# A two-layer encoder trunk: feed-forward products by Strassen's seven block products, with two of the weight sums made by accumulating DMA

## The chip, the core and the metric

One core of one Trainium2 chip runs the kernel. The number to predict is the device time of one execution in microseconds (us). Before the change three runs took 2454.03, 2454.52 and 2454.72 us; the median, 2454.52 us, is the time before.

Engine names are those of the profile: PE is TensorE with its matmuls, PEld its weight loads, DVE is VectorE, ACT is ScalarE, POOL is GpSimd, SP is SyncE, which issues the DMAs of this kernel.

## What is computed

The reference runs two layers on 512 tokens of width 1024. Cut to what matters here:

```python
D_MODEL, SEQ, DEPTH, D_FF = 1024, 512, 2, 2816

def swiglu(x, w_up, w_down):
    a, b = jnp.split(x @ w_up, 2, axis=-1)
    return (jax.nn.silu(a) * b) @ w_down

for i in range(DEPTH):
    x = layer_norm(ALPHA * x + 0.5 * swiglu(x, ffn1_up[i], ffn1_down[i]), ln1_g[i], ln1_b[i])
    mix = token_mix(x, w_in[i], ...)          # four token mixers, gates, an output product
    x = layer_norm(ALPHA * x + mix, ln2_g[i], ln2_b[i])
    ple = jax.nn.sigmoid(x @ w_ple_gate[i]) * (p[i] @ w_ple[i])
    x = layer_norm(ALPHA * x + 0.5 * swiglu(x, ffn2_up[i], ffn2_down[i]) + ple, ln3_g[i], ln3_b[i])
```

The four SwiGLU feed-forwards (two in each layer) are what the change touches.

## The kernel before

Every dense product is three passes of float32r matmuls: an operand is split into hi = float32r(x), by an ACT cast, and lo = x - hi, by a DVE subtract (`split`, L127 to L129), and lo*hi + hi*lo + hi*hi is accumulated (`mm3`, L112 to L116). Weights come by `weights` (L104): one DMA of 512 KB into a `stage` buffer (three of them), then the split into `whi` and `wlo` (six each).

A feed-forward has 22 blocks of 128 hidden features. For a block the up product makes the a half and the b half, each 8 row blocks x 3 passes with 512 token columns, 48 matmuls in all; `finish` (L318) then makes silu on ACT, the product on DVE (`hm`, L324) and the split into `h`. Blocks are taken in two chunks, of 10 and of 12. After a chunk's up products come its down products, a loop over column halves, in it over pairs of blocks, in it over the four token tiles: a pair costs 48 matmuls with 512 columns too. Their sums are added to the rows `z`. The last down product feeds the layer norm, whose transposes are woven between matmuls.

The order on PE is the order of the program text. On the other engines a scheduler sets the order; each engine runs its own list strictly in that order, and DMAs are issued from SP's list. In the second feed-forward of a layer, `ple` (the per-layer embedding) comes first; it needs `pT`, loaded and split by `load_p`, and the rows `z`, which `load_rows` reads back from the scratch `xs` where the norm before stored them.

Of the kernel before, what the change touches and what calls it, by code (L numbers as in the profile page):

```python
# [26 lines left out]
CHUNKS = ((0, 10), (10, 22))  # L27
T2 = 7
# [49 lines left out]
class Trunk:  # L78
    """Every dense product runs as three float32r passes: an operand x is split exactly into
    hi = float32r(x) and lo = x - hi, and lo*hi + hi*lo + hi*hi is accumulated in float32.  # L80
    Activations are kept feature-major (hi and lo, [feature, token]); residuals and layer norms
    are token-major."""

    def __init__(self, tc, ctx, t):
        self.tc, self.nc, self.t = tc, tc.nc, t
        pool = lambda *a, **k: ctx.enter_context(tc.tile_pool(*a, **k))
        self.const = pool(name="const", bufs=1)
        self.ring = pool(name="ring", bufs=1)
        self.small = pool(name="small", bufs=4)
# [7 lines left out]
        self.st, self.ln = {}, []  # L97
        self.scratch = [self.dram.tile([P, D], F32, tag=f"xs{i}", name=f"xs{i}") for i in range(NT)]
        self.w = Weave()
# [4 lines left out]
    def weights(self, src, n=1024):  # L104
        s = self.ring.tile([P, 1024], F32, tag="stage", name="stage", bufs=3)
        h = self.ring.tile([P, 1024], F32R, tag="whi", name="whi", bufs=6)
        lo = self.ring.tile([P, 1024], F32R, tag="wlo", name="wlo", bufs=6)
        self.nc.sync.dma_start(out=s[:, :n], in_=src)
        self.split(h[:, :n], lo[:, :n], s[:, :n])
        return h, lo  # L110

    def mm3(self, ps, lh, ll, rh, rl, start, stop):  # L112
        mm = self.nc.tensor.matmul
        mm(ps, lh, rl, start=start, stop=False)  # L114
        mm(ps, ll, rh, start=False, stop=False)  # L115
        mm(ps, lh, rh, start=False, stop=stop)  # L116
# [24 lines left out]
    def begin(self, up, fp):  # L141
        """The first two pairs of products, in the order in which their operands arrive."""
        ws = [[self.ring.tile([P, 1024], F32R, tag=q, name=q, bufs=6) for q in ("whi", "wlo")] for _ in range(4)]
        raw = [fp.tile([P, 1024], F32, tag="h", name=f"w0_{q}", bufs=12) for q in range(4)]
        ps = [self.bank("up") for _ in range(4)]
        warm = fp.tile([P, SEQ], F32R, tag="h", name="warm", bufs=12)
        self.nc.vector.memset(warm.bitcast(F32), 0.0)
        for _ in range(12):
            self.nc.tensor.matmul(ps[3], warm[:, :P], warm, start=True, stop=True)
        for kk in range(KD // 2):  # L150
            c = slice(256 * kk, 256 * kk + 256)
            x = fp.tile([P, 2, SEQ], F32, tag="h", name=f"x0_{kk}", bufs=12)

            def weight(q):
                self.nc.sync.dma_start(out=raw[q][:, c], in_=up[q // 2, q % 2][:, c])
# [15 lines left out]
    def constants(self):  # L171
        self.load(self.ident, self.t["ident"])
        self.nc.gpsimd.memset(self.mhalf, -0.5)
        self.trig()

    def trig(self):
# [21 lines left out]
        with self.tc.tile_pool(name="trig", bufs=1) as tp:  # L198
            pi = tp.tile([P, NT], I32, tag="pi", name="pi")
            nc.sync.dma_start(out=pi, in_=t["pos"])  # L200
            fr = tp.tile([P, NF], F32, tag="fr", name="fr")
            nc.sync.dma_start(out=fr, in_=t["freq"].partition_broadcast(P))
            pf = tp.tile([P, NT], F32, tag="pf", name="pf")
            v.tensor_copy(pf, pi)
            mk = lambda n: tp.tile([P, NT, NF], F32, tag=n, name=n)
            r, k, s, e, m = mk("r"), mk("k"), mk("s"), mk("e"), mk("m")
# [15 lines left out]
            # angle = 65536 m + rest, and 65536 m = m (c1 + c2 + c3 + c4) mod 2 pi  # L222
# [39 lines left out]
    def norm(self, z, i, g, b, last):  # L262
# [14 lines left out]
        for j in range(2):  # L277
# [6 lines left out]
            self.split(self.xh[sl], self.xl[sl], ps)  # L284

# [10 lines left out]
    def ffn(self, l, which, res, last):  # L296
        nc, t = self.nc, self.t
        up, dn = t[f"up{which}"][l], t[f"dn{which}"][l]
        with ExitStack() as ctx:
            if which == 2:  # L300
                pp = ctx.enter_context(self.tc.tile_pool(name=f"ple{l}", bufs=1, reuse_waits="tile"))
                pt = self.load_p(l, pp)
            fp = ctx.enter_context(self.tc.tile_pool(name=f"ffn{l}{which}", bufs=1, reuse_waits="tile"))
            z = [fp.tile([P, D], F32, tag=f"z{i}", name=f"z{i}") for i in range(NT)]
            g, b = [fp.tile([P, D], F32, tag=q, name=q) for q in ("lng", "lnb")]

            def load_rows():
                self.load_res(z, res)
                self.load_gb(g, b, l, 1 if which == 1 else 3)

            if l or which == 2:
                load_rows()
            if which == 2:
                self.ple(l, z, pp, pt)
            lead = 2 if which == 1 else 0
            alpha = ALPHA2 if which == 1 else None
            h = {}

            def finish(tt, pa, pb):
                sa = fp.tile([P, SEQ], F32, tag="sa", name="sa", bufs=2)  # L320
                hm = fp.tile([P, SEQ], F32, tag="hm", name="hm", bufs=2)
                ht = fp.tile([P, 2, SEQ], F32R, tag="h", name="h", bufs=12)
                nc.scalar.activation(sa, pa, AF.Silu)  # L323
                nc.vector.tensor_tensor(hm, sa, pb, op=ALU.mult)  # L324
                self.split(ht[:, 0, :], ht[:, 1, :], hm)
                h[tt] = ht

            def accumulate(i, half, ps):
                zs = z[i][:, half * 512:(half + 1) * 512]
                if alpha is not None and first:  # L330
                    nc.vector.scalar_tensor_tensor(zs, zs, alpha, ps, op0=ALU.mult, op1=ALU.add)
                else:
                    nc.vector.tensor_tensor(zs, zs, ps, op=ALU.add)
                if tail:
                    self.stats(z[i], i, half)

            for ci, (k0, k1) in enumerate(CHUNKS):
                first, tail = ci == 0, ci == len(CHUNKS) - 1
                tt = k0
                if first and lead:  # L340
                    if l == 0:
                        ps = self.begin(up, fp)
                    else:
                        ws = [self.weights(up[q // 2, q % 2]) for q in range(4)]
                        ps = [self.bank("up") for _ in range(4)]
                        for c0 in (0, 256):
                            self.ready(c0 // P, c0 // P + 1)
                            for w, p in zip(ws, ps):
                                self.up_mm(p, w, c0, c0 + 256)
                    for q in range(lead):  # L350
                        finish(q, ps[2 * q], ps[2 * q + 1])
                    tt = lead
                while tt < k1:
                    if l == 0 and which == 1 and tt == lead + 2:
                        self.constants()
                        load_rows()
                    ps = []
                    for ab in range(2):
                        w = self.weights(up[tt, ab])
                        p = self.bank("up")  # L360
                        self.up_mm(p, w, 0, SEQ)
                        ps.append(p)
                    finish(tt, *ps)
                    tt += 1
                for half in range(2):
                    ps = [self.bank(f"dn{i}") for i in range(NT)]
                    pairs = list(range(k0 // 2, k1 // 2))
                    late = pairs[-LATE:] if tail and half else []

                    def mm(pr, w, i):  # L370
                        for j in range(2):
                            k = 2 * pr + j
                            s, m = slice(i * P, (i + 1) * P), slice(j * 512, (j + 1) * 512)
                            self.mm3(ps[i], h[k][:, 0, s], h[k][:, 1, s], w[0][:, m], w[1][:, m],
# [561 lines left out]
```

## Time and profile before

| | |
|---|---|
| median of the runs | 2454.52 us |
| span of the profiled execution | 2452.4 us |
| PE busy | 2443.3 us (100%), 10996 matmuls |
| DVE busy | 1083.5 us (44%) |
| ACT busy | 695.5 us (28%) |
| POOL busy | 55.1 us (2%) |
| DMA | 257 MB, mean 105 GB/s |

The span runs from the first to the last instruction of one profiled execution. The execution as it is timed also has some 2.1 us around it: the median is that much longer than the span. Because matmuls are pipelined, a matmul's duration (0.39 us for 512 columns) is longer than the distance from one start to the next; the distance is what adds up to the time. It is read from the number of matmuls in a stretch, or from two starts.

### The profile page before, as it was taken

Reading aid. Unit: us, or ns where it says so; the run is one execution under the profiler, and the core shown is the slowest. Engines: PE = TensorE matmul, PEld = TensorE weight load, DVE = VectorE, ACT = ScalarE, POOL = GpSimd, SP = SyncE. Lnnn points to the kernel's source line nnn. Section 1 sums busy time; section 2 is a strip of 40 time slices with the busy share of each in tenths; the row PEclk is TensorE's granted clock in tenths of the full one; section 3 lists DMA queues with packets and bytes.
Section 4 is the critical chain, followed back from the end, with each engine's and each line's share of the span. In section 5 each row is a group of like instructions: output and inputs, shape, how many; then the busy total and the mean of one; then the engine's idle time right before and its main releaser. Section 6 shows DMA issues by size and latency. Waiting matters only on the chain.

```text
span 2452.4 us, 26924 instructions
## 1 busy us (share of the span) xinstructions
PE 2443.3 (100%) x10996; PEld 1987.5 (81%) x10996; DVE 1083.5 (44%) x1712; ACT 695.5 (28%) x994; POOL 55.1 (2%) x93
## 2 busy tenths in 40 slices
PE   9999999999999999999999999999999999999998
PEld 7888888888888888888888888888888888888886
DVE  6333348545446533333443333485454464333334
ACT  4212214324232322222232222143342323222220
POOL 0000001000000000000000000010000000000000
PEclk9999999999999999999999999999999999999999
DMA  6323324213322533322352333232223234333331
GB/s 235 96 92 95 93 95 130 85 58 103 129 95 103 171 96 96 93 95 95 95 174 93 94 94 95 95 121 85 79 91 129 95 114 161 95 94 95 95 95 52
DMA packets 76939, 257.22 MB, mean 105 GB/s; under 512 B 10384, under 2 KB 13584, under 8 KB 76816
## 3 DMA queue, kind: packets, MB, share of 16 engines
q1 hardware_dynamic: 76816, 255.51, 32.4%
q8 instruction: 86, 1.41, 0.2%
q14 instruction: 37, 0.30, 0.0%
HBM read 242.89 MB, written 12.58 MB: 104 GB/s over the span
## 4 chain that ended last, share of the span: by engine, by line
PE 100%; DVE 0%; issue 0%; DVEq 0%
PE up L114 13%; PE up L115 13%; PE up L116 13%; PE dn L115 7%; PE dn L116 7%; PE dn L114 7%; PE gate L116 5%; PE gate L114 5%; PE gate L115 5%; PE wo L114 1%; PE pg L115 1%; PE wo L116 1%; PE pg L116 1%; PE pg L114 1%; PE wo L115 1%; PE br L116 1%
## 5 line engine op out<-in xcount | busy, mean ns | idle before, releaser
L129 DVE TENSOR_TENSOR wlo<-stage,whi 128x1024 fp32r<-128x1024 f32 (+1 forms) x416 | 505.3, 1215 | 728.9 <-ACT whi L128 728.5
L128 ACT CAST whi<-stage 128x1024 fp32r<-128x1024 f32 (+1 forms) x416 | 431.7, 1041 | 728.3 <-PE up L116 294.2
L114 PE MATMUL up<-xl,whi 128*128 128x512 f32 (+1 forms) x1440 | 562.6, 391 | 0.0
L116 PE MATMUL up<-xh,whi 128*128 128x512 f32 (+1 forms) x1440 | 562.2, 390 | 0.0
L115 PE MATMUL up<-xh,wlo 128*128 128x512 f32 (+1 forms) x1440 | 562.2, 390 | 0.0
L114 PEld LDWEIGHTS up<-xl,whi 128*128 128x128 f32 x1440 | 270.6, 188 | 63.3 <-DVE xl L129 0.6
L116 PEld LDWEIGHTS up<-xh,whi 128*128 128x128 f32 x1440 | 270.5, 188 | 62.5
L115 PEld LDWEIGHTS up<-xh,wlo 128*128 128x128 f32 x1440 | 270.6, 188 | 62.4
L114 PE MATMUL dn<-wlo,h 128*128 128x512 f32 x704 | 278.9, 396 | 0.0
L116 PE MATMUL dn<-whi,h 128*128 128x512 f32 x704 | 277.9, 395 | 0.0
L115 PE MATMUL dn<-whi,h 128*128 128x512 f32 x704 | 277.9, 395 | 0.0
L114 PE MATMUL gate<-xl,whi 128*128 128x512 f32 x512 | 206.0, 402 | 0.0
L116 PE MATMUL gate<-xh,whi 128*128 128x512 f32 x512 | 202.6, 396 | 0.0
L115 PE MATMUL gate<-xh,wlo 128*128 128x512 f32 x512 | 202.5, 396 | 0.0
L324 DVE TENSOR_TENSOR hm<-sa,up 128x512 f32<-128x512 f32 x88 | 60.5, 688 | 226.3 <-PE up L116 226.2
L116 PEld LDWEIGHTS dn<-whi,h 128*128 128x128 f32 x704 | 132.0, 188 | 32.2
L115 PEld LDWEIGHTS dn<-whi,h 128*128 128x128 f32 x704 | 132.1, 188 | 31.8
L114 PEld LDWEIGHTS dn<-wlo,h 128*128 128x128 f32 x704 | 132.0, 188 | 31.7
L323 ACT ACTIVATE sa<-up 128x512 f32<-128x512 f32 x88 | 52.6, 598 | 337.9 <-PE up L116 334.2
L116 PEld LDWEIGHTS gate<-xh,whi 128*128 128x128 f32 x512 | 96.2, 188 | 23.1
L115 PEld LDWEIGHTS gate<-xh,wlo 128*128 128x128 f32 x512 | 96.3, 188 | 21.2
L114 PEld LDWEIGHTS gate<-xl,whi 128*128 128x128 f32 x512 | 96.3, 188 | 21.0
(256 smaller groups left out, 2419.4 us busy)
## 6 DMA issues: line engine op xcount, KB each, us to landing
stage<-up_in SPq DMA_DIRECT2D x172, 512.0 KB, 3.6
stage<-dn_in SPq DMA_DIRECT2D x88, 512.0 KB, 3.6
stage<-wg_in SPq DMA_DIRECT2D x64, 512.0 KB, 3.4
xs<-z SPq DMA_DIRECT2D x20, 512.0 KB, 2.6
z<-xs SPq DMA_DIRECT2D x20, 512.0 KB, 6.8
stage<-wbr_in SPq DMA_DIRECT2D x16, 512.0 KB, 3.3
stage<-wo_in SPq DMA_DIRECT2D x16, 512.0 KB, 3.3
stage<-wpg_in SPq DMA_DIRECT2D x16, 512.0 KB, 3.4
```

Of the source, the lines that this page charges most:

```text
L114: mm(ps, lh, rl, start=start, stop=False)
L115: mm(ps, ll, rh, start=False, stop=False)
L116: mm(ps, lh, rh, start=False, stop=stop)
L128: self.nc.scalar.copy(hi, src)
L129: self.nc.vector.tensor_tensor(lo, src, hi.bitcast(F32), op=ALU.subtract)
L323: nc.scalar.activation(sa, pa, AF.Silu)
L324: nc.vector.tensor_tensor(hm, sa, pb, op=ALU.mult)
```

## The change

For 84 of the 88 blocks' up products (all but the first two blocks of each first feed-forward) and for 18 of the 22 blocks' down products in each feed-forward, the product is cut into 2 x 2 blocks, and seven block products with 256 columns take the place of eight. An up unit (`unit`) has seven products of 4 row blocks x 3 passes, 84 matmuls with 256 columns, where 48 with 512 columns were. A down group has seven products for two token tiles; the same 84 stand for 48 in a pair of blocks.

The block sums of the activations are made by `combine` on DVE and split (in `norm`, `begin` and `finish`); those of the up weights by `up_blocks`: `r` holds A11 and A12; `q` gets A21 twice by a plain DMA from SP, and then A11 and A22 are added to its halves by a DMA with `accum_op=ADD`, issued from POOL; `e` holds A22 and a DVE sum; a last DVE sum goes into `r`. Four splits follow. `dn_blocks` does the same for down weights with two accumulating DMAs. There are four `stage` buffers instead of three, and chunks of 6, 6, 6 and 4 blocks; the last chunk's down product (`down_last`) stays classical. `load_p` moves behind `load_rows`.

```diff
-CHUNKS = ((0, 10), (10, 22))
+CHUNKS = ((0, 6), (6, 12), (12, 18), (18, 22))
...
+    def stage(self):
+        return self.ring.tile([P, 1024], F32, tag="stage", name="stage", bufs=4)
...
+    def up_blocks(self, src):
...
+        r, q, e = self.stage(), self.stage(), self.stage()
+        two = lambda t: t.rearrange("p (b c) -> p b c", b=2)
+        self.load(two(r), src[:, 0:2, :])
+        self.load(two(q), src[:, 2:3, :].to_broadcast([P, 2, 512]))
+        self.load(e[:, :512], src[:, 3, :])
+        self.nc.gpsimd.dma_start(out=two(q), in_=src[:, 0::3, :], accum_op=ALU.add)
+        wr = self.halves(r, 1024)
+        wq = self.halves(q, 1024)
+        v.tensor_tensor(e[:, 512:], q[:, 512:], r[:, :512], op=ALU.add)
+        we = self.halves(e, 1024)
+        v.tensor_tensor(r[:, 512:], r[:, 512:], e[:, 512:], op=ALU.add)
+        wf = self.halves(r[:, 512:], 512)
...
+    def combine(self, t, b12, b21, b22):
...
+        v.tensor_tensor(t[:, 2], b22, b12, op=ALU.subtract)
+        v.scalar_tensor_tensor(t[:, 1], t[:, 0], -1.0, b22, op0=ALU.mult, op1=ALU.subtract)
+        v.scalar_tensor_tensor(t[:, 3], t[:, 1], -1.0, b21, op0=ALU.mult, op1=ALU.subtract)
...
+        product(X, "A11", "B11", True)
+        nc.scalar.copy(sn[:, 0], X)
+        product(Y, "S1", "T1", True)
+        nc.scalar.copy(sn[:, 2], Y)
+        product(X, "S2", "T2", False)
+        nc.scalar.copy(sn[:, 1], X)
+        product(Z, "A12", "B21", True)
+        tt(cc[:, :HT], Z, sn[:, 0], op=ALU.add)
+        product(X, "S3", "T3", False)
+        tt(nb, X, sn[:, 2], op=ALU.add)
+        product(Y, "S4", "B22", False)
+        tt(cc[:, HT:], Y, sn[:, 1], op=ALU.add)
+        product(X, "A22", "T4", False)
...
+            if odd:
+                v.tensor_tensor(f[:, 4], f[:, 1], f[:, 0], op=ALU.subtract)
+                self.combine(f[:, 4:], f[:, 0], f[:, 2], f[:, 3])
+                h[pr] = fp.tile([P, 2, 7, HT], F32R, tag="h", name="hb", bufs=3)
+                self.split(h[pr][:, 0], h[pr][:, 1], f[:, 1:])
...
-                self.ple(l, z, pp, pt)
+                with pool("ple") as pp:
+                    self.ple(l, z, pp, self.load_p(l, pp))
```

How the lists of the engines change is shown at three places. On SP before the embedding of the first layer's second feed-forward, the kernel before has (wple and wpg are the embedding's weights, xs the scratch that the norm stores, wo the weights of the product ahead of it):

```order
L108 DMA stage_5696<-wo_in 128x1024
L108 DMA stage_5900<-wple_in 128x1024
L132 DMA ps__5879<-pT_in 128x1024
L108 DMA stage_5948<-wpg_in 128x1024
L108 DMA stage_5954<-wpg_in 128x1024
```

and the changed kernel, at the same load of pT:

```order
L194 DMA xs2_75<-z2_6917 128x1024
L129 DMA stage_7919<-wpg_in 128x1024
L194 DMA z0_7646<-xs0_73 128x1024
L194 DMA z1_7647<-xs1_74 128x1024
L194 DMA z2_7648<-xs2_75 128x1024
L194 DMA ps__7657<-pT_in 128x1024
L129 DMA stage_7925<-wpg_in 128x1024
```

The load of pT moved from ahead of the norm's stores to behind the third store and the read-back of what it stored.

On DVE at the start of a down phase (up and cc, nb, sX are up results, h and hb the split activations, dn and dX the first down results), the kernel before has at the end of the first chunk of up products:

```order
L129 TENSOR_TENSOR wlo_983<-stage_981,whi_982 128x1024
L324 TENSOR_TENSOR hm_842<-sa_841,up_816 128x512
L129 TENSOR_TENSOR wlo_1013<-stage_1011,whi_1012 128x1024
L129 TENSOR_TENSOR h_843<-hm_842,h_843 128x512
L129 TENSOR_TENSOR wlo_1043<-stage_1041,whi_1042 128x1024
L324 TENSOR_TENSOR hm_911<-sa_910,up_885 128x512
```

and the changed kernel at the end of the second chunk:

```order
L472 SCALAR_TENSOR_TENSOR hf_1894<-sX_1922,cc_1926 128x256
L472 SCALAR_TENSOR_TENSOR hf_1894<-nb_1927,cc_1926 128x256
L191 TENSOR_TENSOR wlo_2142<-stage_2113,whi_2141 128x768
L246 TENSOR_TENSOR hf_1894<-hf_1894 128x256
L247 SCALAR_TENSOR_TENSOR hf_1894<-hf_1894 128x256
L191 TENSOR_TENSOR wlo_2167<-stage_2112,whi_2166 128x768
L248 SCALAR_TENSOR_TENSOR hf_1894<-hf_1894 128x256
L191 TENSOR_TENSOR hb_2025<-hf_1894,hb_2025 128x1792
L521 TENSOR_TENSOR z0_620<-z0_620,dX_2028 128x256
```

Where one subtract of 512 columns stood behind the gating, three sums, two weight subtracts and one subtract of 1792 columns stand now.

On SP and DVE in the middle of an up phase of the changed kernel (stage_2661 and stage_2786 are the q of two units that follow each other), SP has

```order
L194 DMA stage_2660<-up1_in 128x1024
L194 DMA stage_2661<-up1_in 128x2x512
L194 DMA stage_2662<-up1_in 128x512
L194 DMA stage_2785<-up1_in 128x1024
L194 DMA stage_2786<-up1_in 128x2x512
L194 DMA stage_2787<-up1_in 128x512
```

and DVE behind it, for the next unit (stage_2916 to stage_2918):

```order
L191 TENSOR_TENSOR wlo_2802<-stage_2787,whi_2801 128x1024
L294 TENSOR_TENSOR cc_2689<-sY_2686,sn_2688 128x256
L191 TENSOR_TENSOR wlo_2807<-stage_2785,whi_2806 128x512
L191 TENSOR_TENSOR wlo_2924<-stage_2916,whi_2923 128x1024
L472 SCALAR_TENSOR_TENSOR hf_2782<-sX_2685,cc_2689 128x256
L472 SCALAR_TENSOR_TENSOR hf_2782<-nb_2690,cc_2689 128x256
L191 TENSOR_TENSOR wlo_2928<-stage_2917,whi_2927 128x1024
L492 TENSOR_TENSOR hf_2782<-hf_2782 128x256
L144 TENSOR_TENSOR stage_2918<-stage_2917,stage_2916 128x512
```

Three stage buffers a unit are taken where two were, and the split of q (here wlo_2928) stands behind the gating of the unit on PE. The plain load of a q waits in the built program for the count that DVE gives after the subtract of the q before it: it gets that buffer.

## Rows read from the trace of the kernel before

**Rows 1.** The page's part 1: busy time, share, instructions.
```profile
PE 2443.3 (100%) x10996; PEld 1987.5 (81%) x10996; DVE 1083.5 (44%) x1712; ACT 695.5 (28%) x994; POOL 55.1 (2%) x93
```

**Rows 2.** The page's part 4: the chain that ended last, by engine.
```profile
PE 100%; DVE 0%; issue 0%; DVEq 0%
```

**Rows 3.** Busy time by stretch: engines with counts, clock, DMA share, GB/s.
```profile
100.00:150.00 50.00, 50.00 (x216) 40.14 (x215) 16.18 (x17) 11.46 (x13) 0.00 (x0) 1.00 0.30 92
...
1250.00:1300.00 50.00, 50.00 (x216) 40.27 (x215) 17.33 (x19) 13.91 (x18) 0.00 (x0) 1.00 0.35 106
```

**Rows 4.** PE in order of time, layer two's first up product: start, duration.
```profile
1225.19 0.28 PE L114 MATMUL up<-xl,whi 128*128 128x256 f32 x1
...
1226.14 0.28 PE L116 MATMUL up<-xh,whi 128*128 128x256 f32 x1
```

**Rows 5.** PE in order of time where the first down phase starts.
```profile
117.83 0.40 PE L116 MATMUL up<-xh,whi 128*128 128x512 f32 x1
118.06 0.40 PE L114 MATMUL dn<-wlo,h 128*128 128x512 f32 x1
```

**Rows 6.** DVE in order of time at the same place.
```profile
118.27 0.69 DVE L324 TENSOR_TENSOR hm<-sa,up 128x512 f32<-128x512 f32 x1 [2.75 <-PE up L116]
...
120.49 0.68 DVE L129 TENSOR_TENSOR h<-hm,h 128x512 fp32r<-128x512 f32 x1
```

**Rows 7.** DVE groups by form: busy us, mean ns, idle before.
```profile
L129 DVE TENSOR_TENSOR wlo<-stage,whi 128x1024 fp32r<-128x1024 f32 x404 | 493.8, 1223 | 718.4 <-ACT whi L128 718.0
...
L129 DVE TENSOR_TENSOR y<-yT,y 128x256 fp32r<-128x256 f32 x24 | 10.0, 415 | 16.9 <-ACT y L128 16.7
...
L560 DVE SCALAR_TENSOR_TENSOR cn<-mlap,rsrm,gn 128x256 f32<-128x256 f32 x8 | 3.9, 484 | 6.5 <-POOL rsrm L138 6.5
...
L129 DVE TENSOR_TENSOR wlo<-stage,whi 128x768 fp32r<-128x768 f32 x2 | 1.9, 959 | 10.5 <-ACT whi L128 10.5
...
L129 DVE TENSOR_TENSOR wlo<-stage,whi 128x512 fp32r<-128x512 f32 x2 | 1.4, 684 | 0.0
```

**Rows 8.** ACT groups by form.
```profile
L128 ACT CAST whi<-stage 128x1024 fp32r<-128x1024 f32 x404 | 421.7, 1047 | 728.2 <-PE up L116 294.2 <-PE dn L116 286.1 <-issue 70.9
L128 ACT CAST h<-hm 128x512 fp32r<-128x512 f32 x88 | 54.2, 616 | 8.6 <-DVE hm L324 8.6
```

**Rows 9.** SP's issues in order of time: start, duration of the group.
```profile
753.77 0.42 SPq L132 DMA_DIRECT2D ps__5879<-pT_in  x1
757.67 17.83 SPq L108 DMA_DIRECT2D stage<-wpg_in  x4
782.26 12.42 SPq L132 DMA_DIRECT2D xs<-z  x3
```

**Rows 10.** DMA issues: count, KB each, median us from issue to landing.
```profile
stage<-up_in SPq DMA_DIRECT2D x172, 512.0 KB, 3.6
...
xs<-z SPq DMA_DIRECT2D x20, 512.0 KB, 2.6
...
lnb<-ln_b_in SPq DMA_DIRECT2D x6, 512.0 KB, 9.5
...
ps__5879<-pT_in SPq DMA_DIRECT2D x1, 512.0 KB, 5.3
```

**Rows 11.** The tile pw: its matmuls, durations in ns, first and last start.
```profile
L114 PE MATMUL pw<-wlo,ph x32: 393/394/483, 796.1 to 2051.9; 128*128 128x512 f32 x32
```

**Rows 12.** Busy time by stretch where the DMA engines are full (columns as Rows 3).
```profile
1240.00:1245.00 5.00, 5.00 (x45) 5.00 (x44) 1.91 (x2) 2.31 (x3) 0.00 (x0) 1.00 1.01 406
```

**Rows 13.** POOL groups by form.
```profile
L138 POOL TENSOR_TENSOR rsln<-rsln,mhalf 128x1 f32<-128x1 f32 x24 | 22.5, 939 | 2065.8 <-DVE rsln L137 2065.8
```

**Rows 14.** Busy time by stretch at the end of the span.
```profile
2444.00:2448.00 4.00, 0.80 (x4) 0.31 (x2) 3.06 (x7) 0.00 (x0) 0.92 (x1) 1.00 0.34 126
2448.00:2452.00 4.00, 0.00 (x0) 0.00 (x0) 1.33 (x3) 0.00 (x0) 0.00 (x0) 0.56 0.35 131
```

More of the change, by code (lines that the diff above doesn't have):

```diff
@@ new lines, in close_tt, with xop, unit, product @@
+    def close_tt(self):
+        self.tt.close()
+        self.tt = None
+    def xop(self, c):
+        if c[0] == "T":
+            q = int(c[1]) - 1
+            return [(self.th[:, q, k, :], self.tl[:, q, k, :]) for k in range(HK)]
+        r, s = int(c[1]) - 1, int(c[2]) - 1
+        return [tuple(x[:, r * HK + k, s * HT:(s + 1) * HT] for x in (self.xh, self.xl)) for k in range(HK)]
+    def unit(self, w, tp):
+        nc = self.nc
+        X, Y, Z = [self.bank(q, [P, HT]) for q in ("sX", "sY", "sZ")]
+        sn = tp.tile([P, 3, HT], F32, tag="sn", name="sn", bufs=1)
+        cc = tp.tile([P, SEQ], F32, tag="cc", name="cc", bufs=2)
+        nb = tp.tile([P, HT], F32, tag="nb", name="nb", bufs=2)
+        tt = nc.vector.tensor_tensor
+        def product(ps, a, b, first):
+            for k, (rh, rl) in enumerate(self.xop(b)):
+                c = slice(k * P, (k + 1) * P)
+                self.mm3(ps, w[a][0][:, c], w[a][1][:, c], rh, rl, first and k == 0, k == HK - 1,
+                         skip_group_check=True)
+        product(X, "A11", "B11", True)
[11 more added lines that the diff above has]
+        product(X, "A22", "T4", False)
+        return cc, X, nb
@@ L260, in stats, with norm @@
         self.nc.vector.bn_stats(self.st[i][:, half, :], z[:, half * 512:(half + 1) * 512])
-    def norm(self, z, i, g, b, last):
+    def norm(self, z, i, g, b, last, blocks):
         nc = self.nc
@@ L284, in norm @@
             self.split(self.xh[sl], self.xl[sl], ps)
+            if not blocks or i < NT // 2:
+                continue
+            if j == 0:
+                self.w.need(self.ln[i - NT // 2])
+                t = self.temp("xt").rearrange("p (c k n) -> p c k n", c=4, k=HK)
+                sl = (slice(None), slice(0, HK), slice((i - 2) * P, (i - 1) * P))
+                nc.scalar.copy(t[:, 2], ps)
+                nc.vector.tensor_tensor(t[:, 0], self.xl[sl].bitcast(F32), ps, op=ALU.subtract)
+                nc.vector.tensor_tensor(t[:, 0], t[:, 0], self.xh[sl].bitcast(F32), op=ALU.add)
+            else:
+                sl = (slice(None), slice(HK, KD), slice((i - 2) * P, (i - 1) * P))
+                self.combine(t, t[:, 2], self.xh[sl].bitcast(F32), ps)
+                nc.vector.tensor_tensor(t[:, 3], t[:, 3], self.xl[sl].bitcast(F32), op=ALU.subtract)
+                sl = (slice(None), slice(None), slice(None), slice((i - 2) * P, (i - 1) * P))
+                self.split(self.th[sl], self.tl[sl], t)
     def ready(self, *toks):
@@ L297, in ffn @@
         nc, t = self.nc, self.t
[L298 to L305, printed above, removed]
+        v = nc.vector
@@ L307, in load_rows @@
+        up, dn, dnp = t[f"up{which}"][l], t[f"dn{which}"][l], t[f"dnp{which}"][l]
+        pool = lambda n: self.tc.tile_pool(name=f"{n}{l}{which}", bufs=1, reuse_waits="tile")
+        with pool("z") as zp:
+            first_use = l == 0 and which == 1
+            if first_use:
+                scratch = zp.tile([P, D], F32, tag="z3", name="trig")
+            z = []
             def load_rows():
+                z.extend(zp.tile([P, D], F32, tag=f"z{i}", name=f"z{i}") for i in range(NT))
                 self.load_res(z, res)
-                self.load_gb(g, b, l, 1 if which == 1 else 3)
@@ L311, in ffn @@
-            if l or which == 2:
+            if not first_use:
                 load_rows()
             if which == 2:
-                self.ple(l, z, pp, pt)
[L315 to L331, printed above, removed]
-                else:
[L333 to L374, printed above, removed]
-                                     k == k0, k == k1 - 1)
-                    for pr in pairs:
-                        if pr in late:
-                            continue
-                        w = self.weights(dn[pr, half])
-                        for i in range(NT):
-                            mm(pr, w, i)
-                    if late:
-                        ws = [self.weights(dn[pr, half]) for pr in late]
-                        self.ln = []
-                        for i in range(NT):
-                            for pr, w in zip(late, ws):
-                                mm(pr, w, i)
-                            accumulate(i, half, ps[i])
-                            self.ln.append(self.w.spawn(self.norm(z[i], i, g, b, last)))
-                    else:
-                        for i in range(NT):
-                            accumulate(i, half, ps[i])
```

231 lines of the change are left out of this document (198 added, 33 removed).

## The prediction

> **What bounds the kernel now.** I read the page's busy shares first, then the chain that ended last, then the stretches, and only then the groups by form, since the first three decide whether a row of another engine costs anything. The reader should see that PE is busy in the whole span and everything else is under half [rows 1], that the chain of waits is all PE and no other engine's line has a share [rows 2], and that an even 50 us of up products holds 216 matmuls, twice, far apart [rows 3]. So today the time is the number of matmuls times their distance: 50 / 216 = 0.2315 us with 512 columns. DVE and ACT stand between for 16 and 11 us of 50 and cost nothing. The kernel can therefore gain by fewer columns on PE, and it can lose whatever makes PE wait.
>
> **What PE saves.** The trace has a stretch with 256 columns, the start of layer two's first feed-forward. From the first to the ninth matmul there are 8 distances in 0.95 us, 0.1188 us each [rows 4]: slightly more than half of 0.2315. An up unit was 48 x 0.2315 = 11.11 us and becomes 84 x 0.1188 = 9.98 us, 1.13 us less (10%, not the eighth that the count of products promises). There are 84 such units, and 9 pairs of blocks in each of four feed-forwards have the same trade in their down products: 84 + 36 = 120 times 1.13 is 136 us. The built program holds 120 x 84 = 10,080 more matmuls with 256 columns, so the change does cut the products as it says.
>
> **The start of a down phase.** Today the last up matmul starts at 117.83 and the first down matmul at 118.06 [rows 5], although the last block's `hm` is made at 118.27 and its split ends at 120.49 + 0.68 = 121.17 [rows 6]. These 3.3 us are covered: the loop over pairs is outside, and four older pairs keep PE at work. In the changed order the loop over pairs is innermost and a chunk has three: the first down product has 6 matmuls (0.71 us) from older pairs and then needs the last one. The new chain behind the last up product, priced by DVE and ACT rows [rows 7, 8]: gating 2 x 0.48 = 0.97; three sums, 0.42 + 2 x 0.48 = 1.38; two weight subtracts of 768 columns that DVE's order has in between, 1.92; an ACT cast of 1792 columns, by the line through 0.62 (512) and 1.05 (1024), 1.69; the subtract of 1792, by 0.68 and 1.22 likewise, 2.03. That is 7.99 us, less 0.71 of cover and some 0.5 because successive DVE starts overlap: 6.8 us, in 12 down phases 82 us. If the two weight subtracts find a gap elsewhere it is 4.9 us (59), at most 8 (96).
>
> **The load of pT.** Before, it is issued at 753.77 [rows 9] and lands 5.3 us later [rows 10], 37 us ahead of its first matmul at 796.1 [rows 11]. Now it is queued on SP behind the third norm store, the third of three issues over 12.42 us from 782.26, so at about 794.3, and behind the read-back that waits until that has landed (2.6). With the issues between, it starts near 797.9, lands at 803.2 and is cast at 804.3: 8 us late, 9 with the subtract that the second matmul needs. Twice, 18 us. The three weight DMAs that are queued behind it on SP are not late to anything that PE reaches before.
>
> **The loop through q.** This is the term that decides, and no row before shows an accumulating DMA, nor any DMA from POOL. In an up phase a q buffer goes through: plain load, 3.6 us [rows 10]; the sum DMA, A; cast, 1.05; subtract, 1.22; and only then the next unit's q can be loaded into it. One round is 5.87 + A per unit. PE needs 9.98, so A up to 4.1 us is free. What stands behind the waiting q on DVE is everything else of that engine, the Z, nb and Y sums of the running unit included, so nothing runs ahead to make up for it. For A, the ends by rows are 2.6 (the fastest copy of 512 KB) and 9.5 (the slowest median) [rows 10]. I build it from the nearest row: a load of the same 512 KB, 3.6; the destination has to be read as well, 512 KB at the 406 GB/s of full DMA engines [rows 12], 1.3; and POOL needs to make the transfer, for which I take one of its short instructions, 0.9 [rows 13]. A = 5.8 us. The round is then 11.67 us, 1.69 over PE's work. I charge that to 84 units and to half of the 48 sum DMAs of the down phases (four of them share four buffers in 30 us of products, two rounds at a time): 108 x 1.69 = 183 us. Each further 1 us of A costs 108.
>
> The Trainium skill, page "DMA: Bandwidth & Descriptors", section "Anatomy of one DMA", gives 2.0 us + bytes / 436,000 per us for a DMA from POOL, and "Collectives: The Full Stack", section "The bandwidth ceiling", says that an add in the DMA path costs no arithmetic but two source reads. An estimate by these two pages is 2.0 + 2 x 1.2 = 4.4 us, and the sum by it would be some 150 us less than mine. No row of before shows such a DMA, so the trace neither agrees nor disagrees.
>
> **What DVE's load adds.** A unit takes from DVE three subtracts of 1024 (3.67), one of 512 (0.68), two sums of 512 (1.37), three PSUM sums of 256 (1.25) and two gatings (0.97): 7.94 us. Every second unit adds three sums (1.80 with the one of a pair's first rows) and the subtract of 1792 (2.03), on average 1.91. Together 9.85 of 9.98 us [rows 7]: DVE goes from a third to nearly all of an up unit. I take 1 us lost for each of 42 pairs, because the 3.83 us of the second unit stand ahead of weight subtracts that PE waits for, and 5 us for the first feed-forward's start, where the block sums of x are made: 47. The ends are 0 and 42 x 3.83 = 161. ACT has 6.3 us a unit and stays off the path.
>
> **The sum**, against the profiled 2452.4 us: -136 + 82 + 18 + 183 + 47 = +194, 2646 us; with the 2.1 us around the span that the runs have, and rounded up, 2650 us. It assumes the clock's upper level throughout.
>
> **The rivals.** (a) *The sum DMA is hidden.* If A is as short as a plain load, 3.6 us, the round is 9.47 us, inside PE's 9.98. The 183 vanishes, and the 47 shrinks towards 5, since early weights absorb DVE's lumps: 2452.4 - 136 + 82 + 18 + 5 to 47 = 2421 to 2463, plus 2: faster, or at most 0.5% slower. It decides from A = 4.1 down. For it speaks that the DMA engines are a third busy [rows 3]; against it, that the transfer must do more than the plain load in 0.5 us more. (b) *The sum DMA is nearly hidden*: the second read costs its 1.3 us, but POOL's part runs beside it, A = 4.9. Then 108 x 0.79 = 85 stands in place of 183, and 2552 comes out. Nothing in the rows speaks for or against POOL's share. The estimate by the two pages of the Trainium skill lies between (a) and this. (c) *DVE becomes the bound* in the up phases, with A hidden: 161 in place of 47 and 183, 2579. For it speaks 9.85 of 9.98; against it, that PE waits only for some of DVE's instructions, and that the 3.83 us fall in the second unit of a pair alone. (d) *The clock falls.* PE's pauses of 7 us are new. At the end of the span the last matmuls end in the stretch with granted clock 1.00, and the next 4 us show 0.56 [rows 14]: after such a pause PE may run at 1.2 GHz in place of 2.4 for some us. If each of 12 pauses costs 3 us more, 36 us come on top, 2686; a loop that makes PE wait in each unit could add more. It lies inside my range.
>
> **How the numbers follow.** A measurement of this kernel tells 0.2% from no change, 5 us. The forecast, the q loop late by 1 us or more a unit, has 0.62; (b) 0.14; (c) 0.08, and with them (d), which changes only the size; all are slower. (a) has 0.16: about 0.10 faster, 0.03 within 0.2%, 0.03 slower. So faster 0.10, same 0.03, slower 0.87. The range: at the top A = 7.6 gives 2650 + 1.8 x 108 = 2845, and with a fallen clock more, so 2850 leaves out about 0.09; 2455 at the bottom leaves out most of (a), 0.11.
>
> **What would show it.** Right: a sum DMA from POOL with a median landing near 6 us; PE's busy share near 86%, with idle that ends with ACT casts and DVE subtracts of weights in the up phases; starts of an S2 or S1 product late in each unit; a unit of some 12 us from one A11 product to the next; a pause of about 7 us before each of the 12 Strassen down phases; about 9 us before the first `pw` matmul, its releaser the cast of `ph`; DVE busy near 1750 us (6 us more in each of 84 units, 5 in each of 36 pairs). The first step is wrong if the distance with 256 columns is not 0.119 us where PE does not wait. The loop is wrong if the sum DMA lands within 4 us, or if PE's idle sits at the down phases alone; then the time is below 2500. The forecast is wrong on its sign if PE stays busy above 97%.

## The result and the profile after

The changed kernel takes 2947.99 us, median of four runs (2942.69 to 2957.14), against 2454.48 us: 1.2014 times as long, with a 95% interval of 1.1993 to 1.2036. The prediction had the sign and not the size: 2650 us, at most 2850. The profiled execution has a span of 2955.4 us.

Of the page of the changed kernel, part 1, the granted clock of part 2, the chain by engine and the DMA landings, which answer to [rows 1, 2, 10]:

```profile
PE 2486.4 (84%) x15316; PEld 2255.5 (76%) x15316; DVE 1748.5 (59%) x2996; ACT 1019.7 (35%) x1488; POOL 198.4 (7%) x225
...
PEclk8888889999999988888988888899999999888889
...
DMA 3%; PE 2%; DVE 1%; issue 0%; ACT 0%; DVEq 0%; ACTq 0%; POOLq 0%; SPq 0%
...
stage<-up_in SPq DMA_DIRECT2D x172, 512.0 KB, 4.7
...
stage<-up_in POOLq DMA_DIRECT2D x84, 512.0 KB, 7.4
stage<-dn_in POOLq DMA_DIRECT2D x48, 384.0 KB, 5.1
```

PE's share and DVE's busy time are as forecast (86%, 1750 us). The sum DMA lands in 7.4 us where the prediction had 5.8, and the clock is below 1.00 wherever up products run. The chain covers 6% of the span and then loses its thread, so who waits for whom is read from the view of waits (total us, times, longest):

```profile
ACT whi L190 <- DMA stage<-up_in: 497.0, 81, 11.6
DVE stage L144 <- DMA stage<-up_in: 290.0, 56, 9.6
...
PE sX L176 <- ACT sn L284: 262.9, 60, 10.0
...
PE dX L176 <- ACT hb L190: 73.1, 12, 7.2
...
PE dX L176 <- DVE z L521: 46.0, 12, 4.4
...
PE dX L177 <- DVE hb L191: 17.8, 12, 1.5
```

ACT waits 497 us to cast weights that a DMA has not brought, DVE 290 us to add the block sum of q at L144. PE itself waits for `sn` at L284, ACT's copy of the A11 product. That copy is short; it stands in ACT's list behind the cast of the *next* unit's q. One round of q in order of time, from the issue of a plain load to the next one's (start, duration; in brackets the idle time before and its releaser):

```profile
170.56 0.38 SPq L194 DMA_DIRECT2D stage<-up_in  x1
...
175.38 1.20 POOL L141 DMA_DIRECT2D stage<-up_in  x1 [13.27 <-DMA stage<-up_in]
...
184.35 1.04 ACT L190 CAST whi<-stage 128x1024 fp32r<-128x1024 f32 x1 [5.86 <-DMA stage<-up_in]
...
185.43 1.23 DVE L191 TENSOR_TENSOR wlo<-stage,whi 128x1024 fp32r<-128x1024 f32 x1 [5.54 <-ACT whi L190]
186.57 0.42 DVE L246 TENSOR_TENSOR hf<-hf 128x256 f32<-128x256 f32 x1
186.90 0.42 DVE L247 SCALAR_TENSOR_TENSOR hf<-hf 128x256 f32<-128x256 f32 x1
187.24 0.68 DVE L144 TENSOR_TENSOR stage<-stage 128x512 f32<-128x512 f32 x1
...
187.99 0.38 SPq L194 DMA_DIRECT2D stage<-up_in  x1
```

This round takes 17.43 us: 4.82 to POOL's issue, 8.97 to the cast, 1.08 to the subtract, 1.81 through it and two sums of activations to L144, 0.75 to the next issue. I followed all 67 rounds inside the up phases in the same way: the mean is 15.70 us, the median 15.46. In 20 of them L144 stands behind the subtract and two activation sums, as here, and the next load starts 1.0 to 1.4 us after the subtract (once 3.4). In the other 47 L144 runs beside ACT's cast, ahead of the subtract, and the next load starts 0.03 us after the subtract (twice 3.0). From one Z sum (L290) to the next inside a chunk, 68 distances in all, the mean is 14.26 us, the median 14.79. PE's 84 matmuls would need 9.9.

On PE near the end of a down phase, in the round above, at the start of the next down phase and before `pw` (answers to [rows 5, 11]):

```profile
141.41 0.39 PE L176 MATMUL dX<-wlo,hb 128*128 128x256 f32 x1 [4.17 <-DVE z L521]
...
180.97 0.28 PE L178 MATMUL sY<-th,whi 128*128 128x256 f32 x1
185.72 0.39 PE L176 MATMUL sX<-tl,whi 128*128 128x256 f32 x1 [4.48 <-ACT sn L284]
...
234.87 0.28 PE L176 MATMUL dX<-wlo,hb 128*128 128x256 f32 x1
...
235.46 0.28 PE L178 MATMUL dX<-whi,hb 128*128 128x256 f32 x1
242.06 0.58 PE L176 MATMUL dX<-wlo,hb 128*128 128x256 f32 x1 [6.33 <-ACT hb L190]
244.12 0.58 PE L177 MATMUL dX<-whi,hb 128*128 128x256 f32 x1 [1.48 <-DVE hb L191]
...
932.22 0.80 PE L176 MATMUL pw<-wlo,ph 128*128 128x512 f32 x1 [9.79 <-ACT ph L190]
```

The five distances from 234.87 to 235.46 are 0.118 us each, as in [rows 4]. The pause for `hb` and the one for `ph` stand where they were foreseen. The one at 141.41, just ahead of the last product of the phase, was not. DVE shows its cause:

```profile
131.39 0.75 DVE L519 SCALAR_TENSOR_TENSOR z<-z,dX 128x256 f32<-128x256 f32 x2
138.38 0.69 DVE L144 TENSOR_TENSOR stage<-stage 128x512 f32<-128x512 f32 x1 [6.25 <-DMA stage<-up_in]
138.99 0.41 DVE L521 TENSOR_TENSOR z<-z,dZ 128x256 f32<-128x256 f32 x1
```

DVE has come to L144 of the next chunk's first unit and waits for that unit's sum DMA; the additions into z stand behind it, and PE may not write on into dX before they have read it.

The clock behind such a pause, by stretches (columns as [rows 3]):

```profile
180.00:186.00 6.00, 1.52 (x13) 1.32 (x12) 0.57 (x1) 1.59 (x3) 0.00 (x0) 1.00 0.55 150
186.00:190.00 4.00, 4.00 (x23) 4.00 (x23) 2.86 (x6) 1.71 (x2) 0.00 (x0) 0.57 0.22 57
190.00:196.00 6.00, 6.00 (x50) 5.83 (x50) 5.55 (x7) 3.61 (x5) 1.20 (x1) 1.00 0.39 75
```

PE stood still from 181.2 to 185.7; in the 4 us from 186 the clock shows 0.57, so for most of them 1.2 in place of 2.4 GHz, and 23 matmuls run where 34 would; then it is back. Over the span the lower level takes 527 us, and the 1629 matmuls of 256 columns that start in it stand 0.213 us apart (median) in place of 0.117: 156 us of PE's time.

### The profile page after: what moved, and what is told of

Same layout as the page of the kernel before. It is cut to its first block, busy times and chain, and to the rows that moved or that the text cites. A ratio compares the mean times of both kernels' runs of the same rounds, so it can differ in the third digit from the quotient of the medians.

```text
span 2955.4 us, 38609 instructions
## 1 busy us (share of the span) xinstructions
PE 2486.4 (84%) x15316; PEld 2255.5 (76%) x15316; DVE 1748.5 (59%) x2996; ACT 1019.7 (35%) x1488; POOL 198.4 (7%) x225
## 5 line engine op out<-in xcount | busy, mean ns | idle before, releaser
L190 ACT CAST whi<-stage 128x1024 fp32r<-128x1024 f32 (+3 forms) x696 | 639.6, 926 | 1025.8 <-DMA stage<-up_in 497.0
L191 DVE TENSOR_TENSOR wlo<-stage,whi 128x1024 fp32r<-128x1024 f32 (+3 forms) x696 | 740.3, 1068 | 289.3 <-ACT whi L190 284.7
L176 PE MATMUL sX<-tl,whi 128*128 128x256 f32 x1008 | 327.1, 325 | 276.2 <-ACT sn L284 262.9
L176 PEld LDWEIGHTS sX<-tl,whi 128*128 128x128 f32 x1008 | 218.7, 217 | 298.5 <-ACT sn L284 275.2
L177 PE MATMUL sX<-th,wlo 128*128 128x256 f32 x1008 | 311.2, 309 | 3.1 <-DVE wlo L191 3.1
L178 PE MATMUL sX<-th,whi 128*128 128x256 f32 x1008 | 310.3, 308 | 0.0
L176 PE MATMUL dX<-wlo,hb 128*128 128x256 f32 x576 | 179.8, 312 | 119.1 <-ACT hb L190 73.1
L144 DVE TENSOR_TENSOR stage<-stage 128x512 f32<-128x512 f32 x84 | 57.9, 690 | 290.0 <-DMA stage<-up_in 290.0
L177 PEld LDWEIGHTS sX<-th,wlo 128*128 128x128 f32 x1008 | 220.8, 219 | 3.8 <-DVE wlo L191 3.8
L178 PEld LDWEIGHTS sX<-th,whi 128*128 128x128 f32 x1008 | 220.6, 219 | 0.0
L177 PE MATMUL dX<-whi,hb 128*128 128x256 f32 x576 | 177.8, 309 | 17.8 <-DVE hb L191 17.8
L178 PE MATMUL dX<-whi,hb 128*128 128x256 f32 x576 | 175.9, 305 | 0.0
L290 DVE TENSOR_TENSOR cc<-sZ,sn 128x256 f32<-128x256 f32 x84 | 35.6, 424 | 198.0 <-PE sZ L178 198.0
L177 PEld LDWEIGHTS dX<-whi,hb 128*128 128x128 f32 x576 | 124.5, 216 | 21.3 <-DVE hb L191 21.3
L178 PEld LDWEIGHTS dX<-whi,hb 128*128 128x128 f32 x576 | 124.6, 216 | 0.0
```

Of the source, the lines that this page charges most:

```text
L144: v.tensor_tensor(e[:, 512:], q[:, 512:], r[:, :512], op=ALU.add)
L176: mm(ps, lh, rl, start=start, stop=False, **more)
L177: mm(ps, ll, rh, start=False, stop=False, **more)
L178: mm(ps, lh, rh, start=False, stop=stop, **more)
L190: self.nc.scalar.copy(hi, src)
L191: self.nc.vector.tensor_tensor(lo, src, hi.bitcast(F32), op=ALU.subtract)
```

## Experiments

The theory from this profile was that the round of q sets the unit. The rivals were (A) the fallen clock, (B) DVE's load, (C) full DMA engines.

**The up sum left out** (e1).

```diff
-        self.nc.gpsimd.dma_start(out=two(q), in_=src[:, 0::3, :], accum_op=ALU.add)
```

> Leaves out the accumulating DMA of the 84 up units: S3 and S1 are then built from A21 alone (values wrong for these blocks), every other instruction stays. Theory (the round of a q buffer sets the unit: plain load 4.6, wait for POOL 0.6, sum DMA 7.4, cast 1.05, subtract 1.22, block sum 0.68, about 14.4 us a unit measured): without the 8 us the round is 7.5 us, hidden by PE's 9.9, the unit falls to 10 to 10.5 us, the second pause of each down phase (DVE held at L144) goes too: 2948 - 84 x 4.1 - 50 = about 2550 us (2480 to 2620), mean clock above 0.95. Rival A (the fallen clock is the price, whatever makes PE wait): the 12 pauses at the down phases keep the clock low, the time falls by less than 200 us, to 2750 or more. Rival B (DVE is the bound, 9.85 of 9.98 us by the rows of before): the unit stays at 11.5 us or more, 2700 us or more, DVE busy in the up phases above 90%.

Measured: 2510.82 us, 1.0227 (1.0212 to 1.0242) times the kernel before. Its page, part 1 and the waits of two groups of matmuls:

```profile
PE 2340.6 (93%) x15316; PEld 2120.2 (85%) x15316; DVE 1737.3 (69%) x2996; ACT 1028.2 (41%) x1488; POOL 97.3 (4%) x141
...
L175 PE MATMUL sX<-tl,whi 128*128 128x256 f32 x1008 | 290.4, 288 | 6.9 <-DVE nb L291 4.8
...
L175 PE MATMUL dX<-wlo,hb 128*128 128x256 f32 x576 | 169.4, 294 | 101.3 <-ACT hb L189 88.0
```

PE's idle time at sX falls from 276 to 7 us. Inside a chunk the Z sums stand 10.26 us apart. The 68 distances are 3.99 us shorter (271 us), and the 13 that span the end of a chunk 12.8 us each (166), 438 us of the 447 between the two profiled executions (437 between the medians). DVE does the same work and does not hold a unit of 10.1 us (median), so B falls. The low clock shrinks to 154 us although the pauses for `hb` remain.

**The add taken away, the transfer kept** (e2).

```diff
-        self.nc.gpsimd.dma_start(out=two(q), in_=src[:, 0::3, :], accum_op=ALU.add)
+        self.nc.gpsimd.dma_start(out=two(q), in_=src[:, 0::3, :])
```

> The sum DMA of the up units loses its add and becomes a plain copy of the same 512 KB from POOL into the same q buffer, behind the same plain load (S3 and S1 are then A11 and A22 alone). Tells what the add itself costs. If the second source read is the price: landing 7.4 falls to 4 to 5 us, the round to 11.5 to 12, the unit likewise, time near 2948 - 84 x 2.5 = 2740 (2650 to 2800). If the way through POOL's queue and the transfer behind a transfer are the price: landing stays at 6.5 us or more and the time above 2880. Rival A (clock): as the landing goes, but the clock stays under 0.93.

Measured: 2803.59 us, 1.1422 (1.1405 to 1.1439). The DMA's row of the page:

```profile
stage<-up_in POOLq DMA_DIRECT2D x84, 512.0 KB, 5.1
```

Without the add it lands 2.3 us earlier, and the time falls by 144 us, to just above the expected range: 63 us for each 1 us. Two thirds of the 437 us hang on there being a second transfer behind the first at all, one third on its add.

What runs beside the transfer matters too. With no load from SP under way beside it, the add lands in 5.7 and 5.9 us (2 cases), the copy in 4.1 and 4.3 (2). With two loads beside it, the moment at which they are issued decides. POOL's own issuing instruction takes 1.20 us for the add and 0.72 us for the copy. Where both loads were issued after it had ended, the add landed in 5.8 to 6.3 us (12 cases) and the copy in 4.0 to 4.6 (17), although the loads were under way to the end; where the first of them came while it ran, the add took 6.6 to 9.1 (25) and the copy 4.3 to 5.9 (6). No run moved the loads alone, so the reason stays open. Places of the changed kernel show it: the sum at 984.98 with nothing beside it, the plain load of q in the round above, the sum of that round (175.38), 0.99 us behind which SP issues the load of e and then that of r, and the sum of the next round (192.96), where they come 1.34 us and more behind it:

```profile
stage<-up_in POOLq DMA_DIRECT2D x1, 512.0 KB, 5.9
...
stage<-up_in SPq DMA_DIRECT2D x1, 512.0 KB, 4.3
...
stage<-up_in POOLq DMA_DIRECT2D x1, 512.0 KB, 8.9
stage<-up_in SPq DMA_DIRECT2D x1, 512.0 KB, 7.2
stage<-up_in SPq DMA_DIRECT2D x1, 256.0 KB, 6.0
...
stage<-up_in POOLq DMA_DIRECT2D x1, 512.0 KB, 6.0
```

**Two buffers for q** (e3). The copies of X and Y go straight into cc and nb, and nb has one buffer, which frees the 4 KB.

```diff
-        r, q, e = self.stage(), self.stage(), self.stage()
+        r = self.stage()
+        q = self.stage() if tt % 2 else tp.tile([P, 1024], F32, tag="sq", name="sq", bufs=1)
+        e = self.stage()
```

> Every second q gets a buffer of its own (4 KB, made free by letting the X and Y copies be added in place), so that two rounds of q run side by side; all work and all DMAs stay. Theory (round through one buffer): the unit falls from 14.4 to PE's 9.9 or DVE's 10 to 11 us, the sum DMA still lands in 7 us or more: 2948 - 84 x 3.5 = about 2650 (2560 to 2740). Rival B (DVE is the bound): unit 11.5 us or more, 2700 or more. Rival C (the DMA engines or the queue of POOL are full, so that each sum takes its 7.4 us whatever the buffer): landing grows to 9 us or more and the time stays above 2850. Rival A (clock): above 2750.

Measured: 2679.85 us, 1.0908 (1.0887 to 1.0929). Sums by buffer, and what PE still waits for:

```profile
sq<-up_in POOLq DMA_DIRECT2D x42, 512.0 KB, 8.9
stage<-up_in POOLq DMA_DIRECT2D x42, 512.0 KB, 7.2
```

```profile
L178 PE MATMUL sX<-tl,whi 128*128 128x256 f32 x1008 | 305.7, 303 | 130.3 <-ACT cc L285 85.3 <-DVE nb L293 43.9 <-ACT whi L192 0.8
```

All work and all transfers are there, some sums land even later, and 268 us are gone (Z sums 11.54 us apart in place of 14.26): what cost the time is one round after another through one buffer. C falls. The other part of the edit cannot have gained much: in the changed kernel ACT's copies into `sn` wait for PE alone, never for DVE to free `sn`. The ring of four now serves five buffers in two units where it served six, so r and e have more room as well; that was not separated. The unit is longer than the 10 to 11 us expected and meets B's 11.5, but e1 has the same work of DVE in 10.26. What remains at sX is again ACT's copy and DVE's sum behind work on a late q, as the releasers say; no run took that apart.

**PE kept at work in the waits** (e4).

```diff
+        self.spin(Z, n)
         product(X, "S2", "T2", False)
...
+                cc, X, nb = self.unit(w, fp, 16 if tt < k1 - 1 else 0)
...
+                self.spin(acc["Z", 0], 0 if g else 60)
```

> PE gets work that nobody reads: 16 matmuls of 256 columns (1.9 us) ahead of the S2 product in all but the last unit of a chunk, 60 (7 us) ahead of the first down product of a chunk, into a bank that is overwritten later. Theory (the round of q sets the unit, a slow PE hides under it): the low-clock time falls from 529 us to under 250, and the time stays within 2920 to 3010, since PE gets faster only where it has to wait anyway. Rival A (the clock is the price, 160 us of slowed matmuls): the time falls by 80 to 150 us, to 2800 to 2870.

Measured: 2978.31 us, 1.2138 (1.2120 to 1.2156).

```profile
PE 2648.0 (89%) x17124; PEld 2420.5 (81%) x17124; DVE 1743.3 (59%) x2996; ACT 1020.1 (34%) x1488; POOL 198.4 (7%) x225
...
PEclk8999999999999998999998999999999999999999
```

The low clock shrinks from 527 to 339 us, less than I expected, and 1808 more matmuls ran; the kernel is 30 us slower, not 80 to 150 faster. By itself this is a weak test: 506 fewer matmuls of 256 columns start in the low clock, 49 us of the 156, and of the added matmuls only those are free that fall into a wait. The trace of the changed kernel says more. In 58 of the 67 rounds the cast starts within 0.1 us of the landing, the subtract within 0.3 us of the cast's end and the next load within 0.1 us of the end of the last reader: no matmul stands in the round, so a slow PE cannot lengthen it. In the up phases it hides under the wait that made it slow, and A falls as the main cause.

**Sums on the POOL engine** (e5).

```diff
-        self.load(two(q), src[:, 2:3, :].to_broadcast([P, 2, 512]))
+        self.load(q[:, 512:], src[:, 2, :])
-        self.nc.gpsimd.dma_start(out=two(q), in_=src[:, 0::3, :], accum_op=ALU.add)
+        g.tensor_tensor(q[:, :512], q[:, 512:], r[:, :512], op=ALU.add)
+        g.tensor_tensor(q[:, 512:], q[:, 512:], e[:, :512], op=ALU.add)
```

> The up sums are made by two additions of 512 columns on the POOL engine in place of the accumulating DMA; A21 is loaded once, 256 KB. Nothing is left out. Theory (the round of q sets the unit): load 3.9, two additions of 1 to 2 us (no row shows one yet), cast 1.05, subtract 1.22, block sum 0.68, some 9 to 11 us, so the unit falls from 14.4 to 10.3 to 11.5 and the second pause of the down phases goes: 2948 - 84 x 3.4 - 50 = 2610 us (2530 to 2700). Rival D (POOL additions are slow, or slow DVE beside them): an addition of 2.5 us or more, unit 13 or more, above 2780. Rival B (DVE bound): 2700 or more with DVE above 90% in the up phases.

Measured: 2664.91 us, 1.0857 (1.0839 to 1.0875); Z sums 12.02 us apart, a little above the forecast. That is 283 us less than the changed kernel, and no DMA sum is left in the up products. One addition on POOL and the DVE subtract beside it, in order of time:

```profile
1030.53 1.29 POOL L142 TENSOR_TENSOR stage<-stage 128x512 f32<-128x512 f32 x1 [7.74 <-DVE z L523]
...
1030.69 2.21 DVE L193 TENSOR_TENSOR wlo<-stage,whi 128x1024 fp32r<-128x1024 f32 x1
```

The subtract takes 2.21 us where it takes 1.22 alone: it lasts 1 us longer, about what is left of POOL's instruction when it starts. Of the 71 such subtracts of this run that meet an addition, 47 last longer, each by 0.13 or 0.14 us less than what was left of the addition; the other 24 keep their 1.2 us, and there the addition ends 2.4 to 2.5 us after the subtract's start, where it takes 1.3 with no work of DVE beside it. The Trainium skill, page "SBUF — State Buffer", section "SBUF: two separate sides", says that POOL and a DVE instruction with two SBUF inputs lock each other out for a whole instruction; these rows agree.

**The up products undone** (e6): 48 matmuls of 512 columns in a block as before, Strassen's scheme in the down products alone.

```diff
-                w = self.up_blocks(up[tt])
+                ws = [self.weights(up[tt][:, 2 * q:2 * q + 2, :].rearrange("p b c -> p (b c)")) for q in range(2)]
...
-                cc, X, nb = self.unit(w, fp)
+                for w, p in zip(ws, ps):
+                    self.up_mm(p, w, 0, SEQ)
```

> One part undone: the up products are the classical ones of before (48 matmuls of 512 columns, two plain weight loads a block), the down products stay Strassen's, with their accumulating DMAs, and so do the chunks. Theory: no q round, so an up block takes 11.2 us as before; of before's time the down products save 36 x 1.36 = 49 us, the first pause of 12 down phases costs 8.5 us each, 102, pT 20: 2454 - 49 + 102 + 20 = 2527 us (2490 to 2570); the second pause (PE waiting for a sum into z behind L144) is absent; granted clock above 0.95. Rival E (the down sum DMAs hold PE too): waits ahead of dX, dY and dZ above 200 us in total, 2600 or more.

Measured: 2528.79 us, 1.0300 (1.0285 to 1.0316), on the forecast, but because two errors cancel. PE's waits:

```profile
PE dX L176 <- ACT hb L190: 48.7, 12, 4.1
PE pw L176 <- ACT ph L190: 19.4, 2, 9.8
PE dX L177 <- DVE hb L191: 18.9, 12, 1.7
```

Only the pauses for `hb` are left at the down phases (48.7 us for the cast and 18.9 for the subtract, less than the 102 I had put), and no wait behind z. The two sum DMAs of a down group cost nothing that the waits show. Some 30 us more go to the low clock behind these pauses (106 us of the span, 255 slowed matmuls of 256 columns and 23 of 512), which was not in the sum.

**An earlier start of the down phases** (e7; `EARLY` is (0, 1, 3), `part` the matmuls of one product, token tile and list of pairs).

```diff
+                self.split(h[pr][:, 0, :3], h[pr][:, 1, :3], f[:, 1:4])
...
+                self.split(h[pr][:, 0, 3:], h[pr][:, 1, 3:], f[:, 4:])
...
+                early = EARLY if g == 0 else ()
+                for n in early:
+                    for i in range(2):
+                        part(n, i, range(len(prs) - 1))
```

> Only the start of the down phases is changed: hb is split in two pieces (the three plain blocks ahead of the four sums), and the first three products with free banks (B11, T1, B21) run over the two older pairs first, 36 matmuls or 4.2 us, ahead of the last pair. The accumulating DMAs stay. Theory: the first pause of 8.7 us falls to 1 or 2 us, 12 x 7 = 84 us less, the up units stay at 14.4: 2948 - 84 = 2864 us (2830 to 2900). Rival F (the time comes back as a longer wait for the next q, whose round then starts no earlier): under 30 us less, 2920 or more.

Measured: 2891.63 us, 1.1784 (1.1766 to 1.1802): 56 us less, between the two expectations. The 13 distances across a chunk's end are 6.3 us shorter each (81 us), those inside chunks 0.25 longer (17), so part of the gain comes back in the next up units. DVE's wait for the sum at its block sum has grown from 290 us:

```profile
DVE stage L145 <- DMA stage<-up_in: 430.0, 78, 10.3
```

**All three** (e8: e3, e5 and e7 in one kernel, and `load_p` again ahead of `load_rows`).

> The sums on POOL (as e5), every second q with a buffer of its own (as e3) and the early start of the down phases (as e7) together. Theory: units of 10.1 to 10.6 us, first and second pauses nearly gone; from the run without the up sum, 2511 us, the first pauses' 100 us go and some 30 us for POOL's additions come: 2440 us (2390 to 2500), near or below the kernel before. Rival (POOL's additions share something with DVE and slow it): above 2520.

Measured: 2625.32 us, 1.0697 (1.0680 to 1.0713). The forecast failed: Z sums stand 11.54 us apart, no better than with e3 alone, and 1.27 us more than in e1. POOL's additions hold DVE as in e5, but DVE's busy time is only 44 us above e7's (1799.0 against 1755.5), 0.5 us a unit; where the rest goes no run took apart.

**What the runs point to** (e9): e6 with e7's start, `T1` split together with the plain blocks, and without the block sums of x, so that `ps`, `ph` and `pl` get memory of their own.

```diff
-        self.th, self.tl = [p.tile([P, 4, HK, HT], F32R, tag=q, name=q) for q in ("th", "tl")]
...
+                self.split(h[pr][:, 0, :4], h[pr][:, 1, :4], f[:, 1:5])
```

> The version that the runs point to: classical up products (as e6), Strassen's scheme in the down products alone, the split of hb in two pieces (B11, B21, B22, T1 first) and the first down products over the older pairs first (as e7); the block sums of x, which nothing reads then, are left out with their 32 KB, so that pT has room of its own and is loaded early. Theory: from e6's 2529 us the first pauses (74 us) and the low clock behind them (30) go, and pT's 20: 2529 - 74 - 30 + 15 (what is left of the pauses) - 20 = about 2420 (2405 to 2445), faster than before by 0.4 to 2%. If the down groups' own sums or DVE take the place of the pauses: 2455 or more.

Measured: 2425.62 us, 0.9878 (0.9862 to 0.9895): 1.2% less than the kernel before, and 18% less than the changed one.

```profile
PE 2400.9 (99%) x12292; PEld 2020.6 (83%) x12292; DVE 1369.7 (56%) x2392; ACT 784.3 (32%) x1090; POOL 97.8 (4%) x141
...
PEclk9999999999999999999999999999999999999999
...
PE dX L177 <- DVE z L531: 11.7, 13, 1.4
```

PE waits 12 us at dX, for sums into z, and not at all at `pw`. The forecast for this kernel was 2420.

## Why the prediction was right in its sign and wrong in its size

**PE's saving: right.** The distance with 256 columns is 0.118 us, and a unit that waits for nothing takes 10.1 us (e1).

**The start of a down phase: right, and one wait short.** PE waits 73.1 us for the cast of `hb` and 17.8 for its subtract, 91 us where 82 were put. Not foreseen were the 46 us behind z: I had written that everything on DVE stands behind the waiting q, but looked for the price in the units alone, not in the down products whose sums share that list.

**The load of pT: right.** 19.5 us for the two casts, 0.9 for the subtracts, against 18.

**DVE's load: too high.** With the sum DMA gone, e1 keeps all of DVE's work, and its units are within 0.4 us of PE's 9.9: up to 30 us for 84 units, where 47 were put.

**The loop through q: the step that failed.** Its mechanism holds (e1, e3), its size does not: a round was put at 11.67 us and measures 15.70 in the mean of 67, and 183 us stood for what costs 437 (e1 against the changed kernel, the waits behind z and most of the low clock included). The 4.0 us that were missing in a round are, by the means of the same 67 rounds:

- The sum DMA, 7.3 us for 5.8, 1.5 more. 5.8 is what it takes alone (5.7 and 5.9), partly by luck: the copy from POOL lands alone in 4.1 to 4.3 us where 3.6 + 0.9 stood, and the add costs 1.6 to 1.9 where 1.3 stood. Most of the sums run beside the two loads that SP issues behind the q load, many of them while POOL is still issuing: that neighbourhood, visible in the order on SP, was not priced.
- The plain load of q, 4.8 for 3.6, 1.2 more; it never takes less than 4.2. It is the one load that reads 256 KB twice and writes two pieces of 2 KB to a partition; whether that is the reason, no run tells.
- POOL's start behind the landing, 0.6 us, not in the sum.
- What ACT and DVE wait before the cast and the subtract, 0.3 us, not in the sum.
- What stands behind the subtract, 0.5 us. The round was closed at the subtract, and in 47 rounds it ends there; in 20 the block sum at L144 still has to read q, behind two activation sums.

Two more things were off in this term. 41 of the 183 us (24 x 1.69) were charged to the sum DMAs of the down phases, which cost nothing that the waits of e6 show. And 1 us of the landing was put at 108 us of the time; e2 gives 63.

An estimate by the fit in the Trainium skill (page "DMA: Bandwidth & Descriptors", section "Anatomy of one DMA") is 3.2 us for a copy of 512 KB from POOL. The runs show 4.1 and 4.3 alone and 5.1 in the median, and 1.6 to 1.9 more for the add, where the estimate in the prediction had 1.2. The measurement decides: the estimate of 4.4 us for the sum was 3 us short.

**Rivals.** (a), the sum hidden, would not have been faster either: with no sum at all e1 takes 2511 us, not 2421 to 2463, since the pauses for `hb` cost 107 us there (88.0 and 18.5) and the clock behind them some 30 (301 slowed matmuls). (c) is excluded by e1. (d), the clock: 156 us of slowed matmuls where 36 were put, but in the up phases they hide in the waits for q, as the rounds show; behind the pauses of the down phases the low clock does cost, some 30 us in e1 and in e6. The top of the range held A = 7.6 us, so the landing lay inside it; the rest of the round did not.

## What to carry to other kernels

A buffer's round ends with its last reader and starts over with the next load: add up every step of it, with landings as they are beside the loads that the same list issues next, and compare it with the work that is to hide it. If it is longer, a second buffer (268 us here) can be worth as much as a shorter round (144 us without the add, 283 with the sums on POOL). An in-order engine hands a late transfer on to everything that stands behind it, so look through its list for instructions of other phases that PE waits for. A low clock in a loop that waits for something else hides in that wait; behind a pause that nothing covers it comes on top (some 30 us in e6).

## What the runs showed of the hardware

An accumulating DMA of 512 KB from POOL lands 5.7 to 5.9 us after its issue when no load runs beside it, a plain copy in 4.1 to 4.3. Two loads from SP that are issued after POOL's issuing instruction has ended (1.20 us, 0.72 for the copy) leave that nearly as it is: 5.8 to 6.3 and 4.0 to 4.6. If the first of them comes while the instruction runs, the add takes 6.6 to 9.1 and the copy 4.3 to 5.9.

An addition of 128x512 on POOL takes 1.3 us with no work of DVE beside it. Beside a DVE subtract of two SBUF operands the one that is later waits for most of what is left of the other: in e5 the subtract lasts up to 1.1 us longer, or the addition ends 2.4 to 2.5 us after the subtract's start.

In the changed kernel PE fell to half its clock for some us behind most of its waits, with 0.213 us between matmuls of 256 columns in place of 0.117; in e9, with 15 us of waits in all and none above 1.6 us, it did not fall at any of them.
